# A two-layer encoder: the memory of the cross-attention laid out transposed by the host, its row factors through DRAM, its values in products of 512 columns

## The chip, the cores and the metric

The kernel runs on one core of a Trainium2 chip. The metric is the device time of one execution in microseconds (us), and the figure compared is the median over runs. TensorE (PE, matrix products), VectorE (DVE), ScalarE (ACT), GpSimd (POOL) and SyncE (SP, which here only issues transfers) each work through an instruction list of their own and wait for one another through semaphores.

## The reference, cut to what matters

Each of the two layers has a mixer, a cross-attention into 256 memory tokens and a gated MLP. The cross-attention normalises the memory rows with a gain per layer:

```python
def rmsnorm(x, gain):
    y = x * lax.rsqrt(jnp.mean(x * x, axis=-1, keepdims=True) + EPS)
    return y * gain

def memory_cross_attention(h, mem_n, w_q, w_kv, w_o):
    q = (h @ w_q).reshape(b, s, 4, 256) * 256 ** -0.5
    kv = mem_n @ w_kv                       # (256, 2048): keys, then values
    k, v = kv[..., :1024], kv[..., 1024:]   # each as 4 heads of 256
    p = softmax(einsum('bshd,bmhd->bhsm', q, k))
    return einsum('bhsm,bmhd->bshd', p, v).reshape(b, s, 1024) @ w_o

x = x + memory_cross_attention(rmsnorm(x, xattn_norm[i]), rmsnorm(mem, mem_norm[i]), ...)
```

There are 1024 tokens of width 1024, all in float32.

## The kernel before

Every large product is made of three (`mm3`, lines 753 to 758): an operand is split into a high half (`high`, line 669, a copy on ACT that rounds) and a low half (`low`, line 672, a subtraction on DVE), and TensorE adds high by high (L756), high by low (L757) and low by high (L758). So each operand costs a copy on ACT and a subtraction on DVE before TensorE can use it.

`cross(i, ...)` (lines 1488 to 1772) emits layer i's cross-attention. It does not write the work down in a fixed order: it hands operations to a `Plan` (lines 162 to 297), each with an engine, a duration, what it reads and writes and which buffers it takes. TensorE's operations keep the order in which they are added; those of the other engines get a due time, worked back from the TensorE operation that needs them (or given by hand as `late`, relative to TensorE's clock in the plan), and a list scheduler emits them. The pools are part of the plan: six scratch tiles of 128x1024 in SBUF (`scr`), half tiles for the split operands (`half`), two PSUM tiles of 128x1024 (`pA`, "A"), and four PSUM tiles of 128x512 (`pB`, "B"). A turn or a product must wait until its pool has a free tile, which is when the last reader of the tile's former content is through.

The order on TensorE is: the q projection in seven block products per column group f = 0 to 3 (class `Seven`), during which the memory is prepared; then the projection of the memory to keys and values, 16 parts (c, m) of 24 products each, 256 columns wide, c = 0 to 3 for keys and 4 to 7 for values; then, mixed with the later parts, scores of the eight query tiles (24 products of 256 columns into a pA tile) and turns of the tiles' probabilities (eight transposes, the even tiles first); then the products of values with probabilities, with the turns of the odd tiles between them. A score is followed by its maximum on DVE (`biggest`, L1635), four exponentials on ACT (`exp`, L1640), a reciprocal on DVE (L1645) and a scaling on POOL (L1649). A turn writes its eight 128x128 blocks into two pB tiles for even t and into one pA tile for odd t (`plan_turn`, L1657 and L1664), from which a high and a low per half are read.

The list `rest` in `main` (L1732) is the order of scores (numbers), projection parts (`None`) and turns ("t0") after the first seven parts.

The memory in each layer (`plan_memory`, lines 1520 to 1559): the gain row is spread over all partitions by a transfer (`bcast`, L722), each of the two tiles of 128 memory rows is loaded (L1531), squared and summed on ACT with a pA tile as scratch (`row_rstd`, L737), its factor made on POOL (`rstd`, L729 and L731), scaled on DVE (L1537), transposed by eight TensorE transposes into pA (L1543), and read out as high and low halves. The operations for tile 0 are added before item (6, 3) of the q projection, those for tile 1 before item (3, 3).

Beside all this the stage prepares work for the MLP: `down_sums` (lines 1775 to 1811) loads blocks of the down weights (L1783), subtracts them on DVE (L1789) and stores the results to DRAM tiles `Wt` (L1792). W_o's weights are loaded from line 1755 on and split ahead of the output projection.

Of the kernel before, what the change touches and what calls it, by code (L numbers as in the profile page):

```python
# [630 lines left out]
class Kernel:  # L631
# [849 lines left out]
    def memory_part(self, mT, g, t):  # L1481
        return (self.R.hv(h).rearrange("p (k n) -> p k n", k=4)[:, :, t * P:(t + 1) * P] for h in mT[2 * g:2 * g + 2])

# [4 lines left out]
    def cross(self, i, X, steps=None, mixer=None, over={}):  # L1488
# [31 lines left out]
        def plan_memory(plan, ts):  # L1520

            def gain():
                mem["gain"] = self.bcast(a["mem_norm"][i])
            if 0 in ts:
                plan.add("load", 1, gain, (), ["mgain"], [("scr", "mgain")])
            for t in ts:
                h, bank = f"mem{t}", ("mturned", t)

                def fetch(t=t):
                    mem[t] = self.scr()  # L1530
                    nc.sync.dma_start(out=mem[t], in_=a["mem"][0][t * P:(t + 1) * P, :])  # L1531

                def square(t=t):
                    mem["r", t] = self.row_rstd(mem[t])

                def norm(t=t):
                    nc.vector.scalar_tensor_tensor(mem[t], mem[t], mem["r", t], mem["gain"], op0=OP.mult, op1=OP.mult)  # L1537

                def turn(t=t):
                    p = self.psA()  # L1540
                    mem["ps", t] = [p[:, :512], p[:, 512:]]
                    for b in range(NK):
                        nc.tensor.transpose(mem["ps", t][b // 4][:, b % 4 * P:(b % 4 + 1) * P],  # L1543
                                            mem[t][:, b * P:(b + 1) * P], self.ident)

                def part(g, j, t=t):
                    if "T" not in mem:
                        mem["T"] = R.get_halves(2)
                    hi, lo = self.memory_part(mem["T"], g, t)
                    src = mem["ps", t][g].rearrange("p (a b) -> p a b", a=4)  # L1550
                    self.low(hi, lo, src) if j else self.high(hi, src)
                plan.add("load", 1, fetch, (), [h], [("scr", h)])
                plan.add("square", 1024, square, [h], [("r", h)], [("A", ("junk", t))], [h, ("junk", t)])
# [34 lines left out]
        def plan_part(plan, c, m):  # L1588
# [5 lines left out]
            def emit():  # L1594
# [10 lines left out]
                if (c, m) == (7, 1):  # L1605
                    R.put_half(*mem.pop("T"))
# [860 lines left out]
```

## Time and profile before

| | |
|---|---|
| median of 3 runs | 2404.05 us (2403.09 to 2405.60) |
| the profiled execution | 2404.15 us |
| its span | 2402.4 us |
| mean granted clock of TensorE | 0.998 |
| TensorE busy | 2381.8 us, 99% of the span |
| VectorE busy | 1863.8 us, 78% |
| ScalarE busy | 1202.7 us, 50% |
| DMA | 322.94 MB, mean 134 GB/s |

The profile is of one execution. A row of a timeline gives the start and duration in us, the engine, the line of the kernel, the operation, what it writes and reads by the program's names, and in brackets how long its engine had been idle before it and what ended the wait. Matmuls are pipelined, so the distance between two starts is what one costs, while the duration is longer. In a list of groups, the number behind x is the count, then come the busy time in us and the mean of one in ns. Layer 0's cross-attention lies at about 460 to 690 us of the span, that of layer 1 ends at about 1670.

### The profile page before, as it was taken

To read this page: it belongs to the slowest core of one execution; us is meant where nothing else is said; L and a number is where in the kernel's file an instruction comes from. 1 tells how busy PE (TensorE), PEld (TensorE's weight loads), DVE (VectorE), ACT (ScalarE), POOL (GpSimd) and SP (SyncE) were. 2 spreads that over 40 slices of the span, in tenths; PEclk is the share of its full clock that TensorE was granted. 3 is DMA by queue.
4 is the path that set the end of the run, shared out by engine and by line. 5 is a ranking of instruction groups with operands and counts; after the bars stand their busy time and mean duration, and the time that the engine had idled before them with its cause. 6 is when DMAs were issued, how large, how long until landed. Compare 5 with 4: busy or idle time off the path is not lost.

```text
span 2402.4 us, 32664 instructions
## 1 busy us (share of the span) xinstructions
PE 2381.8 (99%) x11880; PEld 1903.3 (79%) x11880; DVE 1863.8 (78%) x2609; ACT 1202.7 (50%) x1997; POOL 405.3 (17%) x394
## 2 busy tenths in 40 slices
PE   9999999999999999999999999999999999999998
PEld 7774444688998888888888888898888888888887
DVE  6668998559863798888887768986389888888875
ACT  6545556436552555554554426555255555545442
POOL 4567777410110000000000003011000000000001
PEclk9999999999999999999999999999999999999999
DMA  7000001425951233333387533695124333438752
GB/s 255 1 1 15 15 19 41 163 79 202 319 182 54 88 107 113 110 88 110 107 295 238 193 96 127 220 333 192 62 75 126 94 110 88 120 123 275 253 188 101
DMA packets 323293, 322.94 MB, mean 134 GB/s; under 512 B 32596, under 2 KB 253628, under 8 KB 323132
## 3 DMA queue, kind: packets, MB, share of 16 engines
q1 hardware_dynamic: 323132, 320.85, 41.0%
q8 instruction: 94, 1.54, 0.3%
q14 instruction: 67, 0.55, 0.1%
HBM read 233.30 MB, written 82.64 MB: 132 GB/s over the span
## 4 chain that ended last, share of the span: by engine, by line
PE 92%; issue 3%; DVE 2%; POOL 2%; DMA 1%; ACT 1%; SPq 0%; POOLq 0%; DVEq 0%; ACTq 0%
PE pB L756 23%; PE pB L758 23%; PE pB L757 23%; PE pO L1329 4%; PE pT L1287 3%; PE pA L758 3%; PE pA L756 3%; PE pA L757 3%; PE pS L802 2%; PE pB L325 1%; PE pS L1367 1%; PE pA L2343 1%; DVE R L672 1%; POOL scr L1343 0%; DMA scr<-in_x 0%
## 5 line engine op out<-in xcount | busy, mean ns | idle before, releaser
L757 PE MATMUL pB<-R,R 128*128 128x512 f32 (+1 forms) x2732 | 1029.6, 377 | 0.2 <-DVE R L672 0.2
L756 PE MATMUL pB<-R,R 128*128 128x512 f32 (+1 forms) x2668 | 1010.6, 379 | 2.1 <-DVE R L672 0.9
L758 PE MATMUL pB<-R,R 128*128 128x512 f32 (+1 forms) x2664 | 1003.5, 377 | 1.3 <-DVE R L672 1.2
L757 PEld LDWEIGHTS pB<-R,R 128*128 128x128 f32 x2732 | 514.3, 188 | 93.6 <-DVE R L672 1.2
L756 PEld LDWEIGHTS pB<-R,R 128*128 128x128 f32 x2668 | 502.2, 188 | 98.6 <-issue 3.6
L758 PEld LDWEIGHTS pB<-R,R 128*128 128x128 f32 x2664 | 501.3, 188 | 95.0 <-DVE R L672 3.1
L669 ACT ACTIVATE R<-scr 128x512 fp32r<-128x512 f32 (+3 forms) x376 | 269.3, 745 | 230.2 <-DMA scr<-Gs 59.0
L672 DVE TENSOR_TENSOR R<-scr,R 128x512 fp32r<-128x512 f32 (+2 forms) x332 | 284.0, 884 | 24.5 <-ACT R L669 24.2
L729 POOL TENSOR_SCALAR ms<-ss 128x1 f32<-128x1 f32 x52 | 12.8, 246 | 1624.4 <-ACT R L737 1279.1
L672 DVE TENSOR_TENSOR R<-X,R 128x512 fp32r<-128x512 f32 x258 | 174.8, 685 | 48.4 <-ACT R L669 48.0
L669 ACT ACTIVATE R<-X 128x512 fp32r<-128x512 f32 x258 | 160.8, 630 | 98.2 <-PE pB L757 48.3
L439 ACT COPY scr<-pB 128x512 f32<-128x512 f32 x156 | 91.2, 585 | 180.2 <-PE pB L758 173.0
L808 DVE TENSOR_REDUCE nm<-pS 128x1 f32<-128x512 f32 x232 | 148.2, 682 | 21.8 <-PE pS L802 19.7
L1294 ACT ACTIVATE X<-pT 128x1024 f32<-128x1024 f32 x128 | 124.9, 1023 | 73.3 <-PE pT L1287 71.5
L756 PE MATMUL pA<-R,R 128*128 128x512 f32 (+1 forms) x420 | 150.6, 359 | 0.0
L758 PE MATMUL pA<-R,R 128*128 128x512 f32 (+1 forms) x420 | 150.2, 358 | 0.0
L757 PE MATMUL pA<-R,R 128*128 128x512 f32 (+1 forms) x420 | 149.9, 357 | 0.0
L1329 PE MATMUL pO<-X,XV 128*64 128x512 f32 x512 | 124.1, 605 | 0.5 <-ACT X L1294 0.5
L2034 DVE TENSOR_TENSOR X<-pB,X 128x512 f32<-128x512 f32 (+1 forms) x109 | 74.6, 685 | 63.3 <-PE pB L758 62.3
L441 DVE TENSOR_TENSOR scr<-pB,scr 128x512 f32<-128x512 f32 x156 | 106.7, 684 | 11.0 <-PE pB L758 10.8
L669 ACT ACTIVATE R<-pB 128x256 fp32r<-128x256 f32 (+1 forms) x139 | 63.1, 483 | 86.1 <-PE pB L758 43.3
L1287 PE MATMUL pT<-R,R 64*128 64x512 f32 x768 | 104.2, 394 | 0.0
(234 smaller groups left out, 2910.2 us busy)
## 6 DMA issues: line engine op xcount, KB each, us to landing
Gs<-X SPq DMA_DIRECT2D x105, 256.0 KB
X<-in_ffn_w_up SPq DMA_DIRECT2D x51, 512.0 KB
scr<-in_ffn_w_down SPq DMA_DIRECT2D x45, 512.0 KB
scr<-Gs SPq DMA_DIRECT2D x35, 512.0 KB
scr<-in_xattn_w_kv SPq DMA_DIRECT2D x32, 512.0 KB
scr<-Gs SPq DMA_DIRECT2D x42, 384.0 KB
XV<-in_ffn_w_up SPq DMA_DIRECT2D x31, 512.0 KB
Wt<-scr SPq DMA_DIRECT2D x44, 256.0 KB
```

Of the source, the lines that this page charges most:

```text
L439: self.nc.scalar.copy(out, p)
L441: self.nc.vector.tensor_tensor(out=out, in0=p, in1=out, op=OP.add)
L669: self.nc.scalar.activation(hi, src, AF.Copy)
L672: self.nc.vector.tensor_tensor(out=lo, in0=src, in1=hi.bitcast(F32), op=OP.subtract)
L756: mm(out, ah, bh, start=start, stop=False)
L757: mm(out, ah, bl, start=False, stop=False)
L758: mm(out, al, bh, start=False, stop=stop)
L808: nc.vector.tensor_reduce(NM[G][:, 2 * n + x.start:2 * n + x.stop], S, axis=AX.X, op=OP.max, negate=True)
L1287: nc.tensor.matmul(T[G, kt % 2][:, x * 512:(x + 1) * 512], left, right, start=first and (i, j) == (0, 0), stop=shifted or (not first and i ...
L1294: nc.scalar.activation(E[G, kt], T[G, kt % 2], AF.Exp)
L1329: nc.tensor.matmul(O[G][x * HD:(x + 1) * HD], V32[kt // 4][:, kt % 4, m // 4 * 2 + x], E[G, kt][:, x * 512:(x + 1) * 512], start=kt == 0, ...
L2034: nc.vector.tensor_tensor(out=x, in0=banks[b][:, c], in1=x, op=OP.add)
```

## The change

The host now lays the memory out transposed (`memt`: two tiles of 128 x 1024, features on the partitions, four groups of 256 memory rows side by side) and the memory gains as columns (`mgain`, 128 x 2 x 8).

In layer 0 the memory rows are still loaded and squared (onto themselves), but only for the row factors: two stores of 128x1 put them into a DRAM tile `mrow` of 256 values. In both layers one transfer spreads `mrow` over the partitions, the two tiles of `memt` are loaded, and DVE scales each in four steps of 128x256 in place: by the gain, which is now a factor per partition, and by the spread row. From there the high and low halves are read directly, 1024 wide. The memory's PE transposes, its scaling by rows, and in layer 1 its loading by rows and its squares are gone. All of the memory's operations are added at item (6, 3).

The value projection has four parts of 512 columns in place of eight of 256, with its weights in four pieces a column group instead of two. `rest` now has scores in pairs with a value part between them, and the turn of tile 2 uses a pA tile like those of the odd tiles. The places at which `plan_sums` is called are renumbered to the same five or six.

```diff
-        def plan_memory(plan, ts):
-            def gain():
-                mem["gain"] = self.bcast(a["mem_norm"][i])
...
-                def norm(t=t):
-                    nc.vector.scalar_tensor_tensor(mem[t], mem[t], mem["r", t], mem["gain"], op0=OP.mult, op1=OP.mult)
-                def turn(t=t):
-                    p = self.psA()
-                    mem["ps", t] = [p[:, :512], p[:, 512:]]
-                    for b in range(NK):
-                        nc.tensor.transpose(mem["ps", t][b // 4][:, b % 4 * P:(b % 4 + 1) * P],
-                                            mem[t][:, b * P:(b + 1) * P], self.ident)
...
+        def plan_memory(plan):
+            late = None if i == 0 else -6.0
+            def gains():
+                self.mgain = self.cst.tile([P, 2, NK], F32, name="mgain")
+                self.mrow = self.tc.dram_tile([MEM], F32, name="mrow")
+                nc.sync.dma_start(out=self.mgain, in_=a["mgain"])
+            if i == 0:
+                plan.add("load", 0.5, gains, (), ["mgain"])
+                for t in range(2):
...
+                    def square(t=t):
+                        mem["r", t] = self.row_rstd(mem[t], mem[t])
+                    def store(t=t):
+                        nc.sync.dma_start(out=self.mrow[t * P:(t + 1) * P], in_=mem.pop(("r", t)))
...
+            def spread():
+                mem["row"] = self.bcast(self.mrow)
+            rd = [("rd", t) for t in range(2)] if i == 0 else []
+            plan.add("load", 0.5, spread, rd, ["mrow"], [("scr", "mrow")])
+            for g in range(2):
...
+                def scale(b, g=g):
+                    x = mem["t", g][:, b * MEM:(b + 1) * MEM]
+                    nc.vector.scalar_tensor_tensor(x, x, self.mgain[:, i, 4 * g + b:4 * g + b + 1], mem["row"], op0=OP.mult, op1=OP.mult)
+                def part(j, g=g):
+                    if "T" not in mem:
+                        mem["T"] = R.get_halves(2)
+                    hi, lo = (R.hv(x) for x in mem["T"][2 * g:2 * g + 2])
+                    self.low(hi, lo, mem["t", g]) if j else self.high(hi, mem["t", g])
...
-            plan.add("product", 12.4, emit, ws + [("mT", t, g) for t in range(2) for g in range(2)], [b], [("B", b)], [b, *ws],
+            n, per = (512, 2) if wide else (256, 4)
+            plan.add("product", 24 * n / 512, emit, ws + [("mT", g) for g in range(2)], [b], [("B", b)], [b, *ws],
...
-            banks = [("pturned", t, t % 2 * 2 or g) for g in range(2)]
+            whole = t % 2 or t == 2
+            banks = [("pturned", t, 2 if whole else g) for g in range(2)]
...
-            order, parts = U.order(nf), [(c, m) for c in range(8) for m in range(2)]
+            order, parts = U.order(nf), [(c, m) for c in range(6) for m in range(2)]
...
-                if item in ((6, nf - 1), (3, nf - 1)):
-                    plan_memory(plan, [int(item[0] == 3)])
+                if item == (6, nf - 1):
+                    plan_memory(plan)
...
-            rest = (0, None, 2, None, 4, None, 6, None, 1, None, 3, None, 5, "t0", None, 7, "t2", None, "t4", "t6")
+            rest = (None, 0, 2, None, 4, 6, None, 1, 3, "t0", 5, 7, "t2", None, "t4", "t6")
```

In the changed kernel the scaling is line 1554, the query split's line 1514 is 1511, the maximum 1647, the exponential 1652, the reciprocal 1657 and the turn 1677. Outside the two cross-attentions every engine's list is as before. Three places in the lists of instructions, as the engine's list of instructions has them, tile numbers included, with what an instruction waits for:

VectorE, layer 1, in the last column group of the q projection, where the first scaling of the memory goes in; `XV` and `X` hold blocks of query weights, `R` halves. Before:

```order
L672 TENSOR_TENSOR R_72<-X_1706,R_72 128x512
L395 TENSOR_TENSOR XV_101<-X_1708 128x512 [waits DMAHW4_49]
L1514 SCALAR_TENSOR_TENSOR R_81<-scr,R_81 128x1024 [waits Activation_49]
L672 TENSOR_TENSOR R_72<-XV_101,R_72 128x512 [waits Activation_49]
L395 TENSOR_TENSOR XV_101<-XV_101,X_1706 128x512
```

and now:

```order
L672 TENSOR_TENSOR R_83<-X_1706,R_83 128x512
L395 TENSOR_TENSOR XV_101<-X_1708 128x512 [waits DMAHW1_49]
L1554 SCALAR_TENSOR_TENSOR scr<-scr,mgain 128x256 [waits DMAHW6_49,DMAHW2_49]
L1511 SCALAR_TENSOR_TENSOR R_79<-scr,R_79 128x1024 [waits Activation_49]
L672 TENSOR_TENSOR R_83<-XV_101,R_83 128x512 [waits Activation_49]
```

A scaling that waits for two transfers (the spread row and the tile of `memt`) now stands ahead of the query split and of the low.

TensorE, layer 0, from the last score (tile 7) to the turn of tile 2, whose probabilities are in `X_1706`. Before:

```order
L756 MATMUL pA<-R_72,R_71 128x256
L757 MATMUL pA<-R_72,R_71 128x256
L758 MATMUL pA<-R_72,R_71 128x256
L1664 MATMUL pB<-ident,X_1706 128x128 [waits DVE_49,Pool_49]
L1664 MATMUL pB<-ident,X_1706 128x128
```

and now:

```order
L756 MATMUL pA<-R_85,R_77 128x256
L757 MATMUL pA<-R_85,R_77 128x256
L758 MATMUL pA<-R_85,R_77 128x256
L1677 MATMUL pA<-ident,X_1706 128x128 [waits DVE_49,Activation_49,Pool_49]
L1677 MATMUL pA<-ident,X_1706 128x128
```

The turn's target is pA instead of pB, and it waits for ScalarE as well.

VectorE, layer 0, from the last reads of the scores to the lows of tiles 4 and 6; `R_71` and `R_76` in the second piece are halves of W_o, `R_77` and `R_74` are the last value lows, and the even query tiles' lows go, first half and second half, to R_84 and R_75 before, to R_82 and R_69 now. The first two of these are tile 2's. Before:

```order
L1635 TENSOR_REDUCE nm_6488<-pA 128x4 [waits PE_49]
L672 TENSOR_TENSOR R_84<-pB,R_70 128x4x128 [waits Activation_49]
L672 TENSOR_TENSOR R_75<-pB,R_74 128x4x128 [waits Activation_49]
L672 TENSOR_TENSOR R_77<-pB,R_77 128x256 [waits Activation_49]
L672 TENSOR_TENSOR R_84<-pB,R_70 128x4x128 [waits Activation_49] x2
L672 TENSOR_TENSOR R_75<-pB,R_74 128x4x128
```

and now:

```order
L672 TENSOR_TENSOR R_82<-pA,R_72 128x4x128 [waits PE_49,Activation_49]
L672 TENSOR_TENSOR R_69<-pA,R_67 128x4x128
L672 TENSOR_TENSOR R_71<-scr,R_71 128x1024 [waits DMAHW2_49,Activation_49]
L672 TENSOR_TENSOR R_76<-scr,R_76 128x1024 [waits DMAHW5_49,Activation_49]
L672 TENSOR_TENSOR R_74<-pB,R_74 128x512 [waits Activation_49]
L672 TENSOR_TENSOR R_82<-pB,R_72 128x4x128 [waits Activation_49]
L672 TENSOR_TENSOR R_69<-pB,R_67 128x4x128 [waits Activation_49]
L672 TENSOR_TENSOR R_82<-pB,R_72 128x4x128 [waits Activation_49]
```

Two lows of W_o now come between tile 2's lows and the last value low, and tile 4's second low ahead of tile 6's first.

On SP's queue in layer 0 the new transfers stand behind the stores of the second block of down sums: the two stores of `mrow` (each waits for POOL), two loads of down weights, the spread (it waits for both stores), the first tile of `memt`, and behind these the next sums' stores and the key weights.

More of the change, by code (lines that the diff above doesn't have):

```diff
@@ L1561, in plan_weights @@
+                bs = [(h, b) for b in range(4)]
+                plan.add("copy", 1024, partial(part, 0), [h, *bs], [k], uses=[h], late=late, room=("mT", 4))
+                plan.add("add", 1024, partial(part, 1), [h, k, *bs], [k], uses=[h], late=late)
         def plan_weights(plan, key, src, late=None):
@@ L1674, in part @@
                     self.low(hi, lo, src[:, ks]) if j else self.high(hi, src[:, ks])
[L1675 removed]
+            plan.add("turn", 8, emit, both(t), sorted(set(banks)), [("A", banks[0])] if whole else [("B", k) for k in banks])
             for g in range(2):
```

88 lines of the change are left out of this document (43 added, 45 removed).

## The prediction

> **What bounds the kernel now.** I read the head of the profile page and its chain of waits first, then the busy time by stage, then TensorE's waits, and last single rows where the change touches.
>
> ```profile
> span 2402.4 us, 32664 instructions
> PE 2381.8 (99%) x11880; PEld 1903.3 (79%) x11880; DVE 1863.8 (78%) x2609; ACT 1202.7 (50%) x1997; POOL 405.3 (17%) x394
> PE 92%; issue 3%; DVE 2%; POOL 2%; DMA 1%; ACT 1%; SPq 0%; POOLq 0%; DVEq 0%; ACTq 0%
> ```
>
> TensorE is busy for 99% of the span and carries 92% of the chain. Next, the two stretches that the change touches, layer 0's and layer 1's cross-attention (window, PE, PEld, DVE, ACT and POOL busy, granted clock, DMA share, GB/s):
>
> ```profile
> 560.00:700.00 140.00, 140.00 (x929) 128.45 (x928) 111.51 (x160) 75.73 (x161) 19.68 (x36) 1.00 0.81 285
> 1515.00:1660.00 145.00, 145.00 (x952) 132.81 (x951) 118.37 (x170) 78.19 (x164) 20.72 (x36) 1.00 0.83 291
> ```
>
> TensorE does not pause there, at a clock of 1.00, while VectorE works 80% of the time and the DMA engines 81 to 83%. So what leaves TensorE's list comes off the time, what leaves VectorE's or ScalarE's does not, and a new wait of TensorE comes on top in full. The profiled execution took 2404.15 us, 1.75 above its span; the median of the three runs is 2404.05, so both give the same answer to 0.1 us.
>
> **Work that leaves TensorE.** Starts of matmuls in the timeline give their price, since they overlap (start, duration):
>
> ```profile
> 600.97 0.39 PE L758 MATMUL pB<-R,R 128*128 128x512 f32 x1
> 601.65 0.39 PE L758 MATMUL pB<-R,R 128*128 128x512 f32 x1
> 601.88 1.03 PE L1543 MATMUL pA<-ident,scr 128*128 128x128 f32 x8
> 602.98 0.40 PE L757 MATMUL pB<-R,R 128*128 128x512 f32 x1
> 663.03 0.28 PE L758 MATMUL pA<-R,R 128*128 128x256 f32 x1
> 663.39 0.28 PE L758 MATMUL pA<-R,R 128*128 128x256 f32 x1
> 663.51 0.28 PE L756 MATMUL pB<-R,R 128*128 128x256 f32 x1
> ```
>
> Three 512-wide products take 601.65 − 600.97 = 0.68, or 0.227 each; three 256-wide ones 663.39 − 663.03 = 0.36, or 0.120. A layer's value projection was 8 parts of 24 products of 256, 192 × 0.120 = 23.04; it becomes 4 parts of 24 of 512, 96 × 0.227 = 21.76. Saved: 1.28 a layer, **2.56** in all. The key parts stay as they are.
>
> The eight transposes of a memory tile and one 512-wide product (L756, which the rows leave out) fill 601.88 to 602.98, 1.10, so the eight cost 1.10 − 0.23 = 0.87. There are four such groups (two tiles, two layers): **3.49**. With nothing else changed the run would take 2404.15 − 6.05 = 2398.10.
>
> A rule to weigh against the first of these: the Trainium skill, "TensorE: Matmul & The Clock Gate", section "Back-to-back issue gap", gives an isolated matmul N/2.4 + 2.5 ns, an estimate of 109.2 ns for 256 columns and 215.8 for 512. By it a pair of narrow products saves 2.6 ns where the rows say 13.3, and the sum would keep 0.5 us of the 2.56. The trace's 120 and 227 ns disagree with it here; the section itself says that weight loads enter the spacing of a stream.
>
> **Work that moves on the other engines.** ScalarE loses layer 1's two squares, and in each layer its four reads of 512 become two of 1024; VectorE loses the four norms and gains eight scalings of 128x256 a layer.
>
> ```profile
> 626.78 0.42 DVE L672 TENSOR_TENSOR R<-pB,R 128x256 fp32r<-128x256 f32 x1
> 1542.04 1.28 DVE L1537 SCALAR_TENSOR_TENSOR scr<-scr,rs 128x1024 f32<-128x1024 f32 x1
> 1662.42 3.50 DVE L672 TENSOR_TENSOR R<-scr,R 128x1024 fp32r<-128x1024 f32 x3 [0.26 <-ACT R L669]
> ```
>
> The trace has no 128x256 scaling. A quarter of the norm, 0.32, is the lower end; 0.42, what a 128x256 subtraction takes in the first row, is the upper; I take 0.34 each. Sixteen cost 5.4 against the four norms' 5.1; the wide lows cost 1.17 each (3.50/3). All of it lies beside TensorE's work, at nothing, as long as no result comes late. Four places decide that.
>
> **The turn of query tile 2** moves from pB, which has four banks, to pA, which has two and which the scores also use.
>
> ```profile
> L669 ACT ACTIVATE R<-X 128x512 fp32r<-128x512 f32 x258 | 160.8, 630 | 98.2 <-PE pB L757 48.3
> 663.71 1.22 DVE L1635 TENSOR_REDUCE nm<-pA 128x4 f32<-128x1024 f32 x1 [1.27 <-PE pA L758]
> 665.03 0.47 ACT L1640 ACTIVATE X<-pA,nm 128x256 f32<-128x256 f32 x1 [3.61 <-DVE nm L1635]
> 666.40 0.47 ACT L1640 ACTIVATE X<-pA,nm 128x256 f32<-128x256 f32 x1
> ```
>
> A score's last product makes way at 663.51, its maximum starts 0.20 later, and its fourth exponential ends at 666.87, 3.36 after. With a tenth for the wake (the gap between the maximum's end at 664.93 and the exponential's start), a pA bank comes back 3.45 after its score. Before, a value product lay between scores. Now tile 2's turn follows score 7 directly and takes the bank of score 5, which ended only one score earlier: 24 × 0.120 = 2.88. TensorE waits 3.45 − 2.88 = **0.57** in each layer, +1.1. The ends: nothing, if the bank freed at the exponential's beginning, and 1.8 a layer if tile 0's two 512-wide copies on ScalarE (0.63 each) come before that exponential; the order puts the exponential first, so I take 0.57. Behind the waiting turn stand the last value part and the turns of tiles 4 and 6, which no engine can replace. Scores 5 and 7 follow the score whose bank they take by 2.88 and a turn of 0.87, 3.75 together, so they have 0.3 in hand.
>
> **The first products of the values** read the lows of tiles 0, 2, 4 and 6.
>
> ```profile
> 686.69 0.69 DVE L672 TENSOR_TENSOR R<-pB,R 128x512 fp32r<-128x512 f32 x1 [0.22 <-ACT R L669]
> 687.66 1.29 DVE L672 TENSOR_TENSOR R<-pB,R 128x512 fp32r<-128x512 f32 x2 [0.29 <-ACT R L669]
> 687.96 0.48 PE L756 MATMUL pB<-R,R 128*128 128x512 f32 x1
> 688.41 0.50 PE L757 MATMUL pB<-R,R 128*128 128x512 f32 x1
> 688.75 0.40 PE L758 MATMUL pB<-R,R 128*128 128x512 f32 x1
> ```
>
> TensorE already lost (0.45 − 0.227) + (0.34 − 0.227) = 0.33 here. Now the last value low ahead of them is 512 wide (0.60 to the next start, 1.29 − 0.69, against 0.34 for a narrow one), and the order puts tile 4's second low ahead of tile 6's first: 0.26 + 0.60 = 0.86 later on VectorE. Its two idle times in the rows, 0.22 + 0.29, can take up 0.51. I take a stall of 0.33 + 0.86 − 0.51 = 0.68 in place of 0.33, **+0.35** a layer, +0.7. Ends: none at all, −0.7, if the two W_o lows now planned between them leave VectorE better fed, and the full 0.86, +1.7.
>
> **Given back in layer 1.** There three W_o lows stood together at 1662.42, and TensorE waited for the low behind them:
>
> ```profile
> 1665.86 0.39 PE L758 MATMUL pB<-R,R 128*128 128x512 f32 x1
> 1666.57 0.50 PE L756 MATMUL pB<-R,R 128*128 128x512 f32 x1 [0.33 <-DVE R L672]
> 1666.91 0.40 PE L757 MATMUL pB<-R,R 128*128 128x512 f32 x1
> ```
>
> It lost 0.71 + 0.34 − 0.454 = 0.59. Two of these lows are now spent ahead of the turns, so this goes: **−0.6**; at worst it stays.
>
> **The row factors through DRAM.** Layer 0 loads the rows, squares them, stores two columns of 128 factors, and reads them back on all partitions before the scaling.
>
> ```profile
> 574.07 0.42 SPq L1531 DMA_DIRECT2D scr<-in_mem  x1
> 580.83 1.03 ACT L737 ACTIVATE pA<-scr 128x1024 f32<-128x1024 f32 x1 [1.30 <-DMA scr<-in_mem]
> 406.02 1.22 DMA inv<-rs
> 407.88 4.03 DMA scr<-inv
> 592.84 0.68 DVE L441 TENSOR_TENSOR scr<-pB,scr 128x512 f32<-128x512 f32 x1
> 611.82 0.28 PE L756 MATMUL pB<-R,R 128*128 128x256 f32 x1
> ```
>
> A loaded tile is there 6.76 after its issue, its factor some 1.7 after that (the square's 1.03 and two short steps of GpSimd), near 582.5. The layer's mixer already makes such a round trip, 1.22 for the store and 4.03 for the spread, so with the queue's other entries the factors lie on all partitions by about 589.5. VectorE's first scaling stands behind the addition at 592.84: 3 us in hand, and with its list laid end to end from there the memory's halves are done about 609.9. The first key product, at 611.82 today, comes 1.74 earlier for two removed groups of transposes, at 610.1, and reads the second half after 12 products of 0.120, at 611.5: 1.6 in hand. The nearest long trip is the load's 6.76 in place of 4.03, which still fits. I take nothing. Against that stands a rule: the Trainium skill, "DMA: Bandwidth & Descriptors", section "Specifications", says that pieces under 512 bytes make the DMA read, modify and write, and the stores here are of 4 bytes; its section "Anatomy of one DMA" puts about 2 us of fixed time on each transfer. By these an estimate of 4 us or more for the two trips still falls within the margin, so the sum would be the same; the trace's 5.25 for the mixer's trip agrees.
>
> In layer 1 only the spread remains.
>
> ```profile
> 1526.33 0.45 SPq L722 DMA_DIRECT2D scr<-in_mem_norm  x1
> 1530.60 1.22 DVE L1514 SCALAR_TENSOR_TENSOR R<-scr,R 128x1024 fp32r<-128x1024 f32 x1
> 1531.73 0.68 DVE L672 TENSOR_TENSOR R<-XV,R 128x512 fp32r<-128x512 f32 x1
> 1533.79 0.39 PE L758 MATMUL pB<-R,R 128*128 128x512 f32 x1
> ```
>
> It takes the gains' place on the queue at 1526.33 and is wanted by the scaling at 1530.60, 4.27 later: 4.03 fits, 6.76 does not. Behind that scaling VectorE holds the query split and the low that TensorE needs at 1533.79; the low ends 1532.41, so it has 1.38 in hand, less 0.34 for the scaling itself. I cost it at nothing; the upper end is a spread of 6.76, 6.76 − 4.27 = 2.5 late, less the 1.0: 1.5.
>
> **Sum:** −2.56 − 3.49 + 1.14 + 0.7 − 0.6 = −4.8, and 2404.15 − 4.8 = **2399.4**, against the median as well.
>
> **The rivals.**
>
> *No new stall.* The bank comes back in time and VectorE catches up: the full 6.05, 2398.1. For it speaks that TensorE's stretches have no wait today; against it, the 3.36 of the exponential's rows.
>
> *The pairs of scores pile up.* Two maxima and two sets of exponentials come at once: scores 5 and 7 wait 0.3 more in each layer (0.6), tile 0's copies come first in one (1.26), and layer 1's spread takes 6.76 (1.5, above). That adds 3.4: about 2402.7.
>
> *The row factors come late in layer 0.* VectorE works in order, and so does the queue of SP, where the spread waits for both stores with the memory's tiles and the key weights behind it. From about 3 us late on, each microsecond is one of TensorE's. With 3 us in hand and 4.8 to lose, the gain is gone at 7.8 late, and at 12.6 the kernel is 0.2% slower; 4-byte stores among transfers that hold the engines at 81% of their time could take it there, if the spread took about four times its 4.03; the time would then be 2409.
>
> *Wide products gain nothing.* If 512 columns cost twice 256, the sum keeps 0.5 of the 2.56: 2401.5. The rows of this trace speak against it, since both spacings come from the same streams. The section on the issue gap named above is its support.
>
> That the change does not do what it says can be left aside for the transposes, which are gone from the list of instructions.
>
> **How the numbers follow.** Forecast 0.50 (its own range 2397.8 to 2401), no new stall 0.20, pile-up 0.18, late factors 0.09, no gain from width 0.03. The range of 2397 to 2405.5 leaves out most of the late factors and the tails. A measurement can tell about 0.2% (4.8 us) from no change, so faster means under 2399.25 and slower over 2408.85. The forecast lies at that bound and gives 0.24 to faster and 0.26 to the same; no new stall gives its 0.20 to faster; pile-up gives 0.17 to the same and 0.01 to slower, width its 0.03 to the same; late factors give 0.02 to the same and 0.07 to slower. That makes faster 0.44, same 0.48, slower 0.08.
>
> **What would show it.** Right: no group of memory transposes, value-projection products at 0.227, a gap of about 0.6 on TensorE at tile 2's turn released by ScalarE's exponential, gaps of about 0.7 together at the first products of the values, none near the old 1665.9. Wrong: waits of VectorE on the first 128x256 scaling that reach TensorE, TensorE idle ahead of the first key product, or a wait at scores 5 or 7.

## The result, and the profile after

The changed kernel takes 2408.35 us (median of 22 runs, 2405.71 to 2411.01) against 2404.22 for the kernel before on the same chips: ratio 1.0016, 95% interval 1.0009 to 1.0022. It was forecast at 2399.4, in a range of 2397 to 2405.5, and came out 4.1 us slower than before. Its profiled execution has a span of 2405.6 us, 3.2 more than before's. The head of its page and its chain of waits:

```profile
span 2405.6 us, 32189 instructions
PE 2377.9 (99%) x11656; PEld 1891.4 (79%) x11656; DVE 1865.9 (78%) x2609; ACT 1200.7 (50%) x1981; POOL 416.3 (17%) x390
PE 85%; DVE 5%; issue 3%; DMA 3%; POOL 2%; ACT 1%; SPq 0%; POOLq 0%; DVEq 0%; ACTq 0%
```

TensorE has 224 matmuls fewer and 3.9 us less to do, yet the span is longer. Its share of the chain fell from 92 to 85%, and DVE and DMA took most of what it lost: TensorE waits where it didn't before. The waits of TensorE (engine, line waited for, us in total, times, longest) name the places:

```profile
PE pB L756 <- DVE scr L441: 4.5, 3, 3.9
...
PE pB L756 <- ACT scr L439: 1.1, 1, 1.1
PE pB L1677 <- DVE R L672: 1.0, 2, 0.5
```

The first was 0.3 us in all before, the other two did not exist. The longest in TensorE's timeline of layer 0:

```profile
592.38 0.39 PE L758 MATMUL pA<-R,R 128*128 128x512 f32 x1
596.63 0.77 PE L756 MATMUL pB<-R,R 128*128 128x512 f32 x1 [3.86 <-DVE scr L441]
597.20 0.63 PE L757 MATMUL pB<-R,R 128*128 128x512 f32 x1
597.62 0.63 PE L758 MATMUL pB<-R,R 128*128 128x512 f32 x1
```

From 592.38 to 596.63 are 4.25 where 0.227 were due: 4.02 lost. And the products behind the pause stand 0.43 apart instead of 0.227, up to about 600.1. That loses another 1.65. VectorE's timeline says what held the read-out L441 back:

```profile
587.97 0.68 DVE L672 TENSOR_TENSOR R<-X,R 128x512 fp32r<-128x512 f32 x1
592.38 0.69 DVE L1803 TENSOR_TENSOR X<-X 128x512 f32<-128x512 f32 x1 [3.73 <-DMA X<-in_ffn_w_down]
593.74 1.42 DVE L1803 TENSOR_TENSOR X<-X,X 128x512 f32<-128x512 f32 x2 [0.66 <-DMA X<-in_ffn_w_down]
...
595.80 0.68 DVE L441 TENSOR_TENSOR scr<-pB,scr 128x512 f32<-128x512 f32 x1
```

VectorE stood still for the down weights of the MLP, which has nothing to do with the memory, and TensorE's read-out stood behind them. The first of these weights left SP's queue at 581.56 (582.11 before; counted from the same product of the q projection, which starts at 540.85 now and at 541.74 before, that is 0.3 us later) and was used 10.8 us after that; before, 8 us after the issue it was there without a wait. What stands ahead of them on SP:

```profile
577.69 2.50 SPq L1806 DMA_DIRECT2D Wt<-X  x4
580.23 1.22 SPq L1536 DMA_DIRECT2D mrow<-rs  x2
581.56 3.29 SPq L1797 DMA_DIRECT2D X<-in_ffn_w_down  x2
589.51 0.33 SPq L722 DMA_DIRECT2D scr<-mrow  x1
```

Right ahead stand the two stores of row factors, issued by 581.45. The spread behind the weights has to wait for both, and SP's waits between 570 and 600 show how long that was (us in total, times, longest):

```profile
SPq L722 <- DMA mrow<-rs: 4.6, 1, 4.6
```

The spread leaves at 589.51, so the stores took about 8 us to land. In the table of stretches the last column is what the DMA engines moved (GB/s), the third from the end TensorE's granted clock:

```profile
580.00:582.00 2.00, 2.00 (x11) 1.65 (x10) 2.00 (x3) 0.40 (x2) 0.52 (x1) 1.00 0.76 264
582.00:584.00 2.00, 2.00 (x11) 1.65 (x10) 1.47 (x3) 1.04 (x2) 0.00 (x0) 1.00 2.17 33
584.00:586.00 2.00, 2.00 (x10) 1.69 (x9) 0.21 (x1) 1.12 (x2) 0.00 (x0) 1.00 0.55 33
...
588.00:590.00 2.00, 2.00 (x11) 1.65 (x10) 0.66 (x2) 0.09 (x1) 0.00 (x0) 1.00 0.45 29
590.00:592.00 2.00, 2.00 (x11) 1.65 (x10) 0.00 (x0) 1.09 (x2) 0.00 (x0) 1.00 0.65 238
596.60:600.20 3.60, 3.57 (x9) 2.88 (x10) 3.60 (x7) 1.11 (x2) 0.00 (x0) 0.53 1.01 312
```

Right behind the stores the throughput falls from 264 GB/s to some 30 and stays there for 8 us, while transfers are outstanding (the share column still counts them). I call this the jam. The last row shows the second loss: after a pause of 4 us TensorE's clock was granted at 0.53 for 3.6 us. The Trainium skill, "TensorE: Matmul & The Clock Gate", section "What's actually happening", says that the clock goes to half after an idle window of about 3.4 us and comes back after as long of work; the rows agree, with 4.02 idle and about 3.5 slow.

### The profile page after: what moved, and what is told of

Its sections match the earlier page's. It is cut to its first block, busy times and chain, and to the rows that moved or that the text cites. A ratio compares the mean times of both kernels' runs of the same rounds, so it can differ in the third digit from the quotient of the medians.

```text
span 2405.6 us, 32189 instructions
## 1 busy us (share of the span) xinstructions
PE 2377.9 (99%) x11656; PEld 1891.4 (79%) x11656; DVE 1865.9 (78%) x2609; ACT 1200.7 (50%) x1981; POOL 416.3 (17%) x390
## 4 chain that ended last, share of the span: by engine, by line
PE 85%; DVE 5%; issue 3%; DMA 3%; POOL 2%; ACT 1%; SPq 0%; POOLq 0%; DVEq 0%; ACTq 0%
PE pB L756 22%; PE pB L758 22%; PE pB L757 22%; PE pO L1329 4%; PE pT L1287 3%; PE pA L758 3%; PE pA L756 3%; PE pA L757 3%; PE pS L802 2%; DVE R L672 2%; DMA scr<-in_ffn_w_down 1%; PE pB L325 1%; ACT R L669 1%; PE pS L1367 1%; DMA X<-in_ffn_w_down 1%
## 5 line engine op out<-in xcount | busy, mean ns | idle before, releaser
L757 PE MATMUL pB<-R,R 128*128 128x512 f32 (+1 forms) x2668 | 1019.5, 382 | 0.2 <-DVE R L672 0.2
L756 PE MATMUL pB<-R,R 128*128 128x512 f32 (+1 forms) x2604 | 1000.2, 384 | 7.0 <-DVE scr L441 4.5
L758 PE MATMUL pB<-R,R 128*128 128x512 f32 (+1 forms) x2600 | 993.0, 382 | 1.3 <-DVE R L672 1.2
L757 PEld LDWEIGHTS pB<-R,R 128*128 128x128 f32 x2668 | 502.5, 188 | 96.0 <-DVE R L672 1.2
L756 PEld LDWEIGHTS pB<-R,R 128*128 128x128 f32 x2604 | 490.4, 188 | 106.0 <-issue 7.6
L758 PEld LDWEIGHTS pB<-R,R 128*128 128x128 f32 x2600 | 489.5, 188 | 98.0 <-DVE R L672 3.1
L672 DVE TENSOR_TENSOR R<-scr,R 128x512 fp32r<-128x512 f32 (+2 forms) x336 | 289.7, 890 | 30.5 <-ACT R L669 28.6
L439 ACT COPY scr<-pB 128x512 f32<-128x512 f32 x156 | 91.2, 585 | 183.2 <-PE pB L758 173.8
L441 DVE TENSOR_TENSOR scr<-pB,scr 128x512 f32<-128x512 f32 x156 | 106.8, 685 | 11.4 <-PE pB L758 11.1
L1893 DVE SCALAR_TENSOR_TENSOR scr<-scr,conv 128x1023 f32<-128x1023 f32 x66 | 84.6, 1282 | 20.8 <-ACT scr L1888 18.9
```

Of the source, the lines that this page charges most:

```text
L439: self.nc.scalar.copy(out, p)
L441: self.nc.vector.tensor_tensor(out=out, in0=p, in1=out, op=OP.add)
L672: self.nc.vector.tensor_tensor(out=lo, in0=src, in1=hi.bitcast(F32), op=OP.subtract)
L756: mm(out, ah, bh, start=start, stop=False)
L757: mm(out, ah, bl, start=False, stop=False)
L758: mm(out, al, bh, start=False, stop=stop)
```

## The experiments

Theory J: the 4-byte stores jam the DMA engines, and all of the loss in layer 0 beyond the forecast follows from that. Rival Q: the stores are innocent; layer 0 now loads 1 MB more, SP waits for the factors, or the scalings on VectorE are too late.

Beside each median, which moves by one or two microseconds between executions, stand two stretches of the TensorE timeline, each from the one execution that was profiled. Where kernels have the same instructions in a stretch they agree to 0.03 us (layer 1 in the changed kernel, `big_pieces`, `apart` and `near`), while the product at which the first stretch starts, behind the same TensorE instructions in every kernel, comes anywhere from 539.6 to 543.7. The stretches run in layer 0 from one product of the q projection (541.74 in before) to the first product of the values (687.96); in layer 1 from the product at 1504.87 to one behind the values (1704.72). All in us, difference to before in brackets; the last column is the ratio to before on the same chip with its 95% interval, estimated from the single runs, so that it is not always the quotient of the medians.

| kernel | layer 0 | layer 1 | median | ratio |
|---|---|---|---|---|
| before | 146.22 | 199.85 | 2404.2 | 1 |
| changed | 151.57 (+5.35) | 197.07 (−2.78) | 2408.35 | 1.0016 (1.0009 to 1.0022) |
| before_stores | 154.73 (+8.51) | 199.82 (−0.03) | 2414.55 | 1.0034 (1.0022 to 1.0047) |
| half_pieces | 153.08 (+6.86) | 199.22 (−0.63) | 2412.69 | 1.0030 (1.0018 to 1.0041) |
| big_pieces | 145.83 (−0.39) | 197.09 (−2.76) | 2403.39 | 0.9990 (0.9981 to 0.9999) |
| apart | 145.85 (−0.37) | 197.08 (−2.77) | 2404.21 | 0.9992 (0.9983 to 1.0001) |
| near | 147.23 (+1.01) | 197.10 (−2.75) | 2404.39 | 0.9994 (0.9985 to 1.0003) |
| on_chip | 145.35 (−0.87) | 197.53 (−2.32) | 2402.15 | 0.9985 (0.9976 to 0.9994) |
| on_chip_t2 | 145.68 (−0.54) | 197.40 (−2.45) | 2403.24 | 0.9990 (0.9981 to 0.9999) |
| on_chip_order | 146.13 (−0.09) | 197.77 (−2.08) | 2404.16 | 0.9995 (0.9987 to 1.0004) |
| memory_only | 145.11 (−1.11) | 198.05 (−1.80) | 2404.01 | 0.9992 (0.9983 to 1.0001) |
| values_only | 146.43 (+0.21) | 198.81 (−1.04) | 2406.48 | 1.0002 (0.9993 to 1.0011) |
| on_chip_turn | 143.92 (−2.30) | 195.58 (−4.27) | 2397.95 | 0.9969 (0.9957 to 0.9980) |

Kernels from before_stores to apart ran beside a before of 2405.56, near to on_chip_order beside 2405.60, the last three beside 2406.35.

### The stores alone, in the kernel before

```diff
 (before; parked[t] is the row factor of memory tile t in layer 0; cut)
                 raws[q] = tiles[1] if tiles else [self.scr() for _ in range(2)]
+                for t, r in list(self.parked.items()) if len(self.parked) == 2 else ():
+                    self.parked.pop(t)
+                    nc.sync.dma_start(out=self.mrow[t * P:(t + 1) * P], in_=r)
```

> The kernel before, with one thing added: layer 0's two stores of 128 row factors (256 pieces of 4 bytes) to a DRAM tile that nobody reads, ahead of the same loads of down weights as in the changed kernel. Theory J (the 4-byte stores jam the DMA engines for 8 to 9 us, about 33 ns a piece, and the loads behind them come late): DMA throughput near zero for 8 us after the stores, VectorE waits for the down weights, TensorE loses 3 to 4 us and then some 1.6 at half its clock, time 2408 to 2411. Rival Q (the stores are innocent; the changed kernel's loads are late because layer 0 moves 1 MB more and the queue waits for the factors): within 1 us of 2404.2.

On SP, and on VectorE behind it:

```profile
582.33 2.77 SPq L1812 DMA_DIRECT2D mrow<-rs  x2
585.55 5.56 SPq L1788 DMA_DIRECT2D X<-in_ffn_w_down  x2
```

```profile
596.92 0.69 DVE L1794 TENSOR_TENSOR X<-X 128x512 f32<-128x512 f32 x1 [6.11 <-DMA X<-in_ffn_w_down]
```

```profile
588.00:590.00 2.00, 2.00 (x10) 1.65 (x9) 1.02 (x2) 0.00 (x0) 0.00 (x0) 1.00 0.38 35
...
592.00:594.00 2.00, 2.00 (x11) 1.58 (x9) 0.00 (x0) 1.05 (x2) 0.00 (x0) 1.00 0.61 31
```

The jam comes with the stores alone, with nothing else of the change in the kernel, and it costs 8.5 us in layer 0, 9.0 in the medians. That is more than the 4 to 7 expected. Of Q's causes the extra megabyte and the scalings are not in this kernel. But SP, which waits for GpSimd ahead of the stores, issues the loads 2.8 us later than before, counted from the product that starts the stretch (585.55 behind 542.40, against 582.11 behind 541.74), so this run alone does not clear the queue. `apart`, below, does.

### Half as many pieces

```diff
-                        nc.sync.dma_start(out=self.mrow[t * P:(t + 1) * P], in_=mem.pop(("r", t)))
+                        r = mem.pop(("r", t))
+                        if t == 0:
+                            nc.sync.dma_start(out=self.mrow, in_=r)
...
```

> The changed kernel, but only tile 0's 128 factors are stored, and the spread reads them twice, so tile 1's factors are left out. J: the jam is half as long, 4 to 5 us, the down weights land near 588 to 589 in place of 592.4 and 593.7, TensorE loses under 1 us there and keeps its clock: 2401 to 2402.5. Q: as the changed kernel, 2408.

```profile
586.00:588.00 2.00, 2.00 (x11) 1.65 (x10) 0.63 (x1) 0.49 (x2) 0.00 (x0) 1.00 0.57 33
590.00:592.00 2.00, 2.00 (x10) 1.65 (x9) 1.29 (x2) 0.63 (x1) 0.00 (x0) 1.00 1.08 37
592.00:594.00 2.00, 2.00 (x11) 1.65 (x10) 0.00 (x0) 0.63 (x1) 0.00 (x0) 1.00 0.26 16
```

A miss. One store was issued at 583.12 and the throughput is still at 16 GB/s ten microseconds later: the jam is not shorter, and layer 0 loses more than in the changed kernel. So a price per piece, as J had it, is wrong. Two things are mixed in here, since the spread was altered as well: it reads the 128 factors twice, in pieces of 512 bytes. In layer 0 it leaves at 592.13, so the last 2 us of low throughput may be its own. In layer 1, where no factors are stored, VectorE waits for it, and that stretch is 2.15 us longer than in the changed kernel:

```profile
DVE scr L1558 <- DMA scr<-mrow: 2.5, 1, 2.5
```

What 256 pieces into 1024 bytes (about 9 us) and 128 pieces into 512 bytes (9 to 10) share is how densely they fall: every 512 bytes of DRAM get 128 pieces, and every smaller place its share. That leads to J2: writes into the same place follow one another, and different places go on side by side. With 512 bytes as the place that is about 9.5 / 128 = 75 ns a write.

### Larger pieces, and the same pieces far apart

```diff
 (big_pieces; mrow is 256 x 128)
+                        nc.sync.dma_start(out=self.mrow[t * P:(t + 1) * P], in_=mem[t][:, :P])
 (apart; mrow is 256 x 128)
+                        nc.sync.dma_start(out=self.mrow[t * P:(t + 1) * P, :1], in_=mem.pop(("r", t)))
...
```

The cut lines of `apart`, and of `near` below, store whole rows of 512 bytes to `mrow` beforehand (two here, eight there), so that the spread has something to read.

> The changed kernel, but the two stores write 128 columns of the squared memory rows in place of the factors, to rows of their own: still 256 pieces, but of 512 bytes, so the row factors are replaced by other numbers. If the size of the pieces makes the jam, it is gone: 2400 to 2401.5. If their number does, or under Q, as the changed kernel: 2408.

> The changed kernel, but each factor's 4 bytes go to a DRAM row of their own, 512 bytes from the next, and the spread reads the first two rows instead, so the factors are replaced by other numbers. If the jam comes from small writes that follow one another into the same few DRAM lines, it is gone or much shorter: 2400 to 2402. If any write of 4 bytes costs as much wherever it goes, 2408, as under Q.

In `apart` the stores were issued at 582.11; the stretches behind them:

```profile
582.00:584.00 2.00, 2.00 (x11) 1.65 (x10) 2.00 (x3) 0.60 (x2) 0.00 (x1) 1.00 0.53 164
584.00:586.00 2.00, 2.00 (x11) 1.65 (x10) 0.95 (x2) 0.52 (x1) 0.00 (x0) 1.00 0.93 213
586.00:588.00 2.00, 2.00 (x11) 1.65 (x10) 0.69 (x1) 1.12 (x2) 0.00 (x0) 1.00 1.00 366
```

Neither has the jam, and layer 0 is the same to 0.02 us: 145.85 and 145.83, 5.7 less than the changed kernel. (In steps of half a microsecond the throughput of `apart` does drop, to 18 and 1 GB/s from 583.0 to 584.0, and that of `big_pieces` to no less than 92; TensorE feels neither.) `apart` has the changed kernel's queue, waits, loads and scalings, so Q falls. And neither the number of pieces nor their 4 bytes as such cost the time, but where they land. Layer 0 was forecast 2.1 us shorter than before (−1.28 − 1.75 + 0.57 + 0.35) and came out 5.35 longer; of these 7.5 the stores explain 5.7, and the waits below the rest. The medians, 2404.2 and 2403.4, are about 2 us over the ranges that were expected. Of that 1.4 is the chip, whose before took 2405.56 instead of 2404.2; the rest is that the expectation had left out those waits.

### Pieces 16 bytes apart

```diff
+                        nc.sync.dma_start(out=self.mrow.rearrange("(a b) -> a b", b=4)[t * P:(t + 1) * P, :1], in_=mem.pop(("r", t)))
```

> The changed kernel with the 256 pieces of 4 bytes laid 16 bytes apart, so that 32 of them fall into 512 bytes of DRAM; the spread reads other numbers in place of the factors. The runs so far: 128 pieces into 512 bytes jammed the DMA engines for 10 us, 256 pieces into 1024 bytes for 9, one piece per 512 bytes not at all. If writes into the same 512 bytes follow one another at 70 to 80 ns each, the jam is 32 x 75 ns = 2.4 us, the loads of down weights come about 2.4 us later than without one, and TensorE waits little: 2403 to 2405. If the stretch that counts is 64 bytes, 4 pieces share one and the jam is 0.3 us: time as with the pieces far apart. If all that counts is the number of pieces, a jam of 9 us and the time of the changed kernel, 2408.

```profile
582.00:584.00 2.00, 2.00 (x10) 1.65 (x10) 1.63 (x3) 0.91 (x2) 0.00 (x0) 1.00 0.40 51
584.00:586.00 2.00, 2.00 (x11) 1.65 (x10) 0.34 (x1) 1.12 (x2) 0.00 (x0) 1.00 0.50 156
586.00:588.00 2.00, 2.00 (x11) 1.65 (x10) 1.12 (x3) 0.63 (x1) 0.00 (x0) 1.00 0.75 242
```

About 2 us of jam, between the 9 of the packed pieces and none: the 2.4 that J2 gave. Layer 0 is 1.4 us over `apart`. That excludes a price per piece (9 us), and places of 16 bytes or less, which would get one piece each, as in `apart`. It does not tell how large the place is: the 0.3 us that was expected for 64-byte places kept the 75 ns, but 16 packed pieces in 64 bytes that take 9.5 us are 0.6 us a write, and four of those are 2.4 us as well. Rows of TensorE show only a short wait, and its clock stays whole:

```profile
592.24 0.39 PE L758 MATMUL pA<-R,R 128*128 128x512 f32 x1
593.62 0.47 PE L756 MATMUL pB<-R,R 128*128 128x512 f32 x1 [0.99 <-DVE scr L441]
593.93 0.39 PE L757 MATMUL pB<-R,R 128*128 128x512 f32 x1
594.16 0.39 PE L758 MATMUL pB<-R,R 128*128 128x512 f32 x1
```

### The factors spread by TensorE

```diff
+                def fill(t=t):
+                    x = mem[t][:, :P]
+                    nc.vector.scalar_tensor_tensor(x, self.ident, 0.0, mem.pop(("r", t))[:, :1].to_broadcast([P, P]), op0=OP.mult, op1=OP.add)
...
+            def turn():
+                p = mem["rows"] = self.psB()
+                for t in range(2):
+                    nc.tensor.transpose(p[:, t * P:(t + 1) * P], mem[t][:, :P], self.ident)
```

> The changed kernel with layer 0's row factors spread by TensorE: VectorE fills a 128x128 tile with each tile's factors, two transposes turn them into one row on all partitions, ScalarE copies it, and one piece of 1 KB goes to DRAM for layer 1. If the 4-byte stores are the whole of the 5.7 us that layer 0 lost beyond its other waits, the jam and the slow clock are gone and the time is 2404.2 - 3 + 0.2 = 2401.4 (2400 to 2402.5), with the waits at tile 2's turn and tile 6's turn (0.67 each in both layers) as in the changed kernel. If the memory's scaling on VectorE was the slower part all along, layer 0 still ends 3 us or more late: 2405 or more.

Measured 2402.15, 3.45 less than before (2.8 less expected); layer 0 6.2 us shorter than in the changed kernel. The same computation without the packed stores is faster than before. The wait for L439 is gone as well; in its place the second product of the first key part waits 0.5.

### Each part of the change alone

```diff
 (memory_only, against before; plan_rows is that of on_chip)
-                if item in ((6, nf - 1), (3, nf - 1)):
-                    plan_memory(plan, [int(item[0] == 3)])
+                if item == (1, nf - 1) and i == 0:
+                    plan_rows(plan)
+                if item == (6, nf - 1):
+                    plan_memory(plan)
 (values_only, against the changed kernel)
-                if item == (6, nf - 1):
-                    plan_memory(plan)
+                if item in ((6, nf - 1), (3, nf - 1)):
+                    plan_memory(plan, [int(item[0] == 3)])
```

> The kernel before with the memory's part alone: transposed by the host, row factors spread by TensorE as in on_chip, values still 256 wide, scores and turns in their old order. If the steps of the sum hold, TensorE loses the 32 transposes (3.5 us), gains two (0.2), and the waits of before stay (0.33 in each layer, 0.83 in layer 1), with 0.5 at the first key product: 2.8 us less than before, ratio 0.9988. If the new order of the scores is what brings the gain, within 1 us of before.

> The kernel before with the other part alone: values 512 wide, the new order of scores and turns, the memory as before. By the sum: 2.56 less for the wide products, 0.83 less for the stall of layer 1 that goes, 2.7 more for the waits at the turns of tiles 2 and 6: 0.7 us less than before, not to be told from no change. If wide products gain nothing, 1.9 us more than before.

`memory_only` puts `on_chip`'s memory into the kernel before; `values_only` puts the memory of before into the changed kernel. The two stretches move by −1.11 and −1.80 (together −2.9, expected −2.8), and by +0.21 and −1.04 (together −0.8, expected −0.7). The medians can't tell either from no change for certain: −2.3, with an interval that just reaches 1, and +0.1. So the wide products do give their 1.28 a layer, which the waits at the turns take back; what `values_only` gains in layer 1 is its old stall, which goes.

### The waits at the turns

In the changed kernel, layer 0, TensorE at the turn of tile 2, then at that of tile 6 and the first values:

```profile
682.02 0.28 PE L758 MATMUL pA<-R,R 128*128 128x256 f32 x1
682.82 1.06 PE L1677 MATMUL pA<-ident,X 128*128 128x128 f32 x8 [0.52 <-issue]
...
691.16 0.63 PE L1677 MATMUL pB<-ident,X 128*128 128x128 f32 x4 [0.50 <-DVE R L672]
...
692.42 0.48 PE L756 MATMUL pB<-R,R 128*128 128x512 f32 x1
692.87 0.50 PE L757 MATMUL pB<-R,R 128*128 128x512 f32 x1
```

0.80 where 0.12 were due: 0.68 lost at tile 2's turn, after ScalarE's last exponential of score 5, which ends at 682.62 in its timeline; forecast were 0.57. The profile names "issue" here and POOL in layer 1, where the row is the same. At tile 6's turn 0.67 are lost, because its second pB tile is the one that the last value part filled, and the low that empties it stands behind two W_o lows on VectorE. At the first values the loss is the 0.33 of before. Two kernels tried to take the turns' waits away:

```diff
 (on_chip_t2)
-            whole = t % 2 or t == 2
+            whole = t % 2
 (on_chip_order)
-            rest = (None, 0, 2, None, 4, 6, None, 1, 3, "t0", 5, 7, "t2", None, "t4", "t6")
+            rest = (0, None, 2, 4, None, 6, 1, None, 3, "t0", 5, None, 7, "t2", "t4", "t6")
```

> As on_chip, with tile 2's turn back in two pB tiles. If its stall is the wait for score 5's exponentials, both layers' 0.67 go: 1.3 us less than on_chip, about 2400. The rival is that the pB banks are then short and the value part or the turns of tiles 4 and 6 wait as long instead: the same as on_chip.

> As on_chip, with the value parts placed so that one lies between scores 5 and 7 and none between the turns of tiles 2 and 4 (order: 0, part, 2, 4, part, 6, 1, part, 3, turn 0, 5, part, 7, turns 2, 4, 6). Tile 2's bank then comes back 5.4 us earlier relative to its turn, and no value part holds a pB bank when tile 6 turns: both waits go in both layers, 2.7 us less than on_chip, about 2398.7. If DVE is what is short there, the wait moves to the first products of the values and grows by as much: the same as on_chip.

In `on_chip_t2` tile 2 turns at once, and the value part behind it waits instead; in `on_chip_order` the waits move to tile 1's turn and the first values:

```profile
679.97 0.47 PE L756 MATMUL pB<-R,R 128*128 128x512 f32 x1 [1.13 <-DVE R L672]
```

```profile
684.54 1.06 PE L1692 MATMUL pA<-ident,X 128*128 128x128 f32 x8 [0.81 <-ACT XV L1667]
686.58 0.47 PE L756 MATMUL pB<-R,R 128*128 128x512 f32 x1 [0.97 <-DVE R L672]
```

Both misses: the rivals held, and the waits were traded. A last kernel put the value part ahead of the turns:

```diff
 (on_chip_turn)
-            rest = (None, 0, 2, None, 4, 6, None, 1, 3, "t0", 5, 7, "t2", None, "t4", "t6")
+            rest = (None, 0, 2, None, 4, 6, None, 1, 3, "t0", 5, 7, None, "t2", "t4", "t6")
```

> As on_chip, with the last value part ahead of tile 2's turn, so that tiles 2, 4 and 6 turn one after another. Tile 2's bank is then free 5.4 us before it is wanted, and tile 6's second bank is the value part's, read 1.7 us before it is wanted: both 0.67 waits go. Rival: VectorE has the value low and three lows of 0.6 to do behind the value part before the second product of the values, and they are late by up to 1 us. Waits of 0.3 per layer there give 2.7 us less than on_chip; a full us gives 1.3 less.

```profile
681.51 1.03 PE L1692 MATMUL pA<-ident,X 128*128 128x128 f32 x8
682.38 1.91 PE L1692 MATMUL pB<-ident,X 128*128 128x128 f32 x16
684.13 1.04 PE L1692 MATMUL pA<-ident,X 128*128 128x128 f32 x8
684.92 0.48 PE L756 MATMUL pB<-R,R 128*128 128x512 f32 x1
685.27 0.50 PE L757 MATMUL pB<-R,R 128*128 128x512 f32 x1
```

Now ScalarE and VectorE have the value part's 5.4 us (24 × 0.227) for what they still hold of the scores and of tile 0's turn. The three turns run through without a wait, and the first values lose 0.12 + 0.10. The two stretches are 1.4 and 2.0 us shorter than in `on_chip`. At 2397.95 against 2406.35 this kernel is the fastest of all, 0.31% under before by the ratio (0.20 to 0.43%).

## Why the prediction was wrong

The sum was −2.56 − 3.49 + 1.14 + 0.7 − 0.6 = −4.8. Against it stand the two stretches, +5.35 − 2.78 = +2.6; the other 0.6 of the spans and 1.5 of the medians lie in stages whose instructions are the same, and I did not follow them up.

- **Work that leaves TensorE (−6.05): right.** `memory_only` and `values_only` together confirm it to about 0.2 us. The rival that wide products gain nothing is refuted: by it `values_only` would have cost 1.9 us, and its stretches gave −0.8. (Its time of 2401.5 was worked out with 0.5 us kept; products at exactly twice the price keep nothing, which gives 2401.9.) The rule of the Trainium skill, "TensorE: Matmul & The Clock Gate", section "Back-to-back issue gap", that would have made the wide products worth 0.5 us in place of 2.56 is not borne out either: by it `values_only` would have cost an estimated 1.4 us.
- **Tile 2's turn (+1.14): right in cause, a little small.** 0.68 and 0.67, so 1.35. That the wait is for the bank is only supported by undoing it: in `on_chip_t2` it went and another came, in `on_chip_turn`, where the bank is free earlier, it went.
- **The first values (+0.7): the wrong place.** They lose what they lost before. The lateness of VectorE shows one step earlier, at tile 6's turn, because the same value low also frees a pB tile that this turn needs; 0.67 a layer, 1.34.
- **Given back in layer 1 (−0.6): right, a little small.** The four pauses of 0.48, 0.11, 0.24 and 0.11 behind the old 1665.86 (the last two ahead of the products at 1668.31 and 1668.64) are gone: −0.95; I had counted the first two.
- **Work beside TensorE (0): one cover failed.** A scaling takes longer than the 0.34 I took (479 ns alone, 0.40 from start to start), and in layer 0 the eighth stands on VectorE behind four subtractions of the down sums. ScalarE's copy L439, which empties a pB tile, writes the scratch tile that the spread row had taken; in ScalarE's list of instructions it waits for the row's transfer and for this scaling, the row's last reader. So ScalarE stands still and TensorE waits for the pB tile. The rows below show it, VectorE's and ScalarE's. It costs 1.26, and 0.11 at the next product. I had laid out VectorE's list up to the key product only, not who takes the row's scratch tile next. The wait is in `apart` and `big_pieces` as well, so the jam does not cause it.
- **The row factors through DRAM (0): the step that failed.** I priced the store by the mixer's, 1.22 us. That one writes an 8x128 tile, eight pieces of 512 bytes; this one writes 256 pieces of 4 bytes into 1 KB, and took about 8 us to land. It cost TensorE 4.02 + 1.65 = 5.67 us: the changed kernel against `apart` shows 5.72. Late factors were one of the rivals, at 9%, but with the wrong mechanism: I asked when the spread would land and counted 3 us in hand for it. That its 2409 lies near the 2408.35 measured is luck. The spread did no harm: it left at 589.51, when the forecast had the factors on all partitions, but VectorE came to its first scaling only at 600.13 and did not wait for it. The loads behind the stores, which have nothing to do with the memory, came late, and VectorE had little in hand for those: in `near`, 2 us of jam already cost TensorE a wait of 1.0 behind VectorE's read-out. None of the three signs of being wrong that I had named appeared; I had looked at the memory's own path alone. Of the rule of the Trainium skill, "DMA: Bandwidth & Descriptors", section "Specifications", on pieces under 512 bytes I noted that it spoke against the stores, and then I took the fixed time per transfer of that page, which its section "Anatomy of one DMA" gives for transfers that GpSimd issues (these come from SP), instead of asking what the pieces do to other traffic.

```profile
609.29 0.48 DVE L1554 SCALAR_TENSOR_TENSOR scr<-scr,mgain 128x256 f32<-128x256 f32 x1
```

```profile
609.85 1.08 ACT L439 COPY scr<-pB 128x512 f32<-128x512 f32 x2 [3.44 <-DVE scr L1554]
```

With these sizes the terms give −6.05 + 1.35 + 1.34 − 0.95 + 1.37 + 5.67 = +2.73, and the stretches +2.6.

## What to carry to other kernels

A small transfer is priced by its own time and by what it does to those behind it: after a store of many small pieces look at the throughput of the next ten microseconds, and at who waits for what was issued then. A column of 128 partitions written to consecutive words of DRAM was the worst case here; two transposes on the busiest engine (0.2 us) were cheaper than a store that cost nobody's time on paper. And where a wait is for a bank, moving one operation trades it for another unless the engines that empty the banks are given time: the order that won puts the longest product just ahead of the turns.

## What the runs showed of the hardware that was not expected

- Writes of 4 bytes packed into the same place of DRAM hold up the DMA engines: 128 of them in 512 bytes for 9 to 10 us, 32 in 512 bytes for about 2, one in 512 bytes for no time that TensorE felt. 256 in 1024 bytes take no longer than 128 in 512, so different places go on side by side. How large a place is the runs leave open, between 16 and 512 bytes; with 512 a write takes about 75 ns, an estimate from these runs. The Trainium skill, "DMA: Bandwidth & Descriptors", section "Specifications", has transfers under 512 bytes read, modify and write. A chain of these on one place would fit the runs, but 256 pieces of 4 bytes apart made layer 0 no longer than 256 of 512 bytes did (145.85 and 145.83), so small pieces as such were not what cost time here.
- The hold-up is general: loads of 4 KB pieces from other addresses, on the same queue, moved at 30 GB/s in place of some 300. Whether stores from another queue would have spared them was not tried.
- TensorE's clock is granted at 0.53 for 3.6 us after a pause of 4.0, and the products stand 0.43 apart; they do so too behind the pauses of 6.9 in `before_stores` and 5.1 in `half_pieces`. After a pause of 1.2 (`near`) they stand 0.23 apart. Where between 1.2 and 4.0 the limit lies no run here shows. The pause of 4.0 cost 1.65 us more than it shows.
